# Low parts of the down projections' weights: subtraction on VectorE against negation and an adding transfer

## The chip, the cores and the metric

The kernel runs on one core of a Trainium2 chip. The metric is the device time of one execution in microseconds (us). A core has five engines with queues of their own: TensorE (PE; its weight loads are listed apart as PEld), VectorE (DVE), ScalarE (ACT), GpSimd (POOL) and SyncE (SP). Sixteen DMA engines serve the core. Each engine works through its own queue in order; semaphores tie the queues together.

## The reference

A decoder trunk of two layers over 256 tokens of width 1024, all in float32. Each layer adds three things to the residual stream `h`, and a final RMSNorm ends it:

```python
for l in range(DEPTH):                                        # DEPTH = 2
    h = h + 0.5 * swiglu(rmsnorm(h, ffn1_norm[l]), ffn1_w_gate[l], ffn1_w_up[l], ffn1_w_down[l])
    u = rmsnorm(h, mix_norm[l])
    z = u @ w_in[l]                                           # columns for three mixers and their gates
    ...                                                       # latent attention, differential attention, pooling
    h = h + merged @ w_out[l]
    h = h + 0.5 * swiglu(rmsnorm(h, ffn2_norm[l]), ffn2_w_gate[l], ffn2_w_up[l], ffn2_w_down[l])
return rmsnorm(h, final_norm)

def swiglu(x, w_gate, w_up, w_down):
    return (jax.nn.silu(x @ w_gate) * (x @ w_up)) @ w_down    # 1024 -> 2816 -> 1024
```

The down projection is the last product, 2816 by 1024. There are four of them: two in each layer.

## The kernel before

**Three products for one.** TensorE multiplies in the type `float32r`, which keeps fewer bits than float32. So each operand is split: `hi` is the value rounded to `float32r`, `lo` is what is left, `value - hi`. A product is made of three matmuls (`mm3`, lines 201 to 203): hi by hi, hi of the activations by lo of the weights (line 202), and lo of the activations by hi of the weights. The second of the three is the first that reads a weight tile's `lo`.

**Weight tiles.** All weights lie in one array, `wall`, in the order of use that `plan()` writes out by hand. A full tile is 4 blocks of 128 rows by 512 columns, in SBUF 128 partitions by 2048 values, 1024 KB. A down projection (names ending in `w_down`) has 22 blocks of rows and two halves of 512 columns: in each half five full tiles and one of two blocks (128 by 1024 values). So one down projection has 12 tiles, and the four have 48.

**The split of a tile** is `wsplit_now`. SyncE's queue loads the tile into `raw` (line 194). ScalarE rounds it into `hi` (line 183). VectorE subtracts, `lo = raw - hi` (line 184). For tiles of the feed-forward networks each of the two is one instruction for the whole tile. The first four tiles of the kernel take a path of their own (the branch `first`) and are no down projection's. `raw`, `hi` and `lo` have three buffers each, so a load waits until the tile three places earlier no longer needs its `raw`, and a cast until TensorE has finished with the `hi` of the tile three places earlier. Loads, casts and subtractions of the coming tiles run ahead of TensorE as far as these rings allow. `ahead()` issues one tile's split before the work behind which it would stand.

**The down projection** runs in `gemm_tokens`: for each half two accumulators of 128 tokens by 512 columns; for each tile four blocks, two token groups and three matmuls, 24 matmuls in a full tile. Its activations are `ghi` and `glo`, so that its matmuls appear in the profile as `acc<-hi,ghi`, `acc<-lo,ghi` and `acc<-hi,glo`. At the end of a half VectorE adds the result to `h` (line 369), and TensorE transposes it for the next norm. The last feed-forward of the kernel has no following norm; there the last two tiles of a half are taken together (`tail=2`), first one token group, then the other.

**GpSimd** has little to do in these stages: at the start of the next one it raises the norm's mean square to the power -1/2 (line 229). No transfer is issued from its queue.

Of the kernel before, what the change touches and what calls it, by code (L numbers as in the profile page):

```python
# [11 lines left out]
F32 = mybir.dt.float32  # L12
# [4 lines left out]
ALU = mybir.AluOpType  # L17
# [71 lines left out]
def trunk(ctx, tc, x, xt, positions, wall, small, lamrow, fnorm, out):  # L89
    nc = tc.nc  # L90
# [52 lines left out]
    def wsrc(spec):  # L143
        _, _, _, nk, _, n = spec
        return wall[offs[spec]:offs[spec] + P * nk * n].rearrange("(p k n) -> p k n", p=P, k=nk)
# [13 lines left out]
    def wsplit(spec):  # L159

        if spec not in pending_splits:
            pending_splits[spec] = wsplit_now(spec)
        return pending_splits.pop(spec)

    def ahead():

        i = order_of[latest[0]] + 1
        if i < len(order_of):
            spec = plan()[i]
            pending_splits[spec] = wsplit_now(spec)  # L170

    def wsplit_now(spec):
        latest[0] = spec
        _, _, _, nk, _, n = spec
        raw = wp.tile([P, nk, n], F32, tag="raw", name="raw")
        hi = wp.tile([P, nk, n], F32R, tag="hi", name="hi")
        lo = wp.tile([P, nk, n], F32R, tag="lo", name="lo")
        first = offs[spec] < 4 * P * 2048
        fl = lambda a: a.rearrange("p k n -> p (k n)")
        rawf, hif, lof = fl(raw), fl(hi), fl(lo)  # L180

        def split(ks):
            nc.scalar.copy(out=hif[:, ks], in_=rawf[:, ks])  # L183
            nc.vector.tensor_tensor(out=lof[:, ks], in0=rawf[:, ks], in1=hif[:, ks].bitcast(F32), op=ALU.subtract)  # L184

        if first:

            for k in range(nk):
                nc.sync.dma_start(out=raw[:, k], in_=wsrc(spec)[:, k])
                split(slice(k * n, (k + 1) * n))  # L190
                if opening:
                    opening.pop(0)()
            return hi, lo
        nc.sync.dma_start(out=raw, in_=wsrc(spec))
        step = nk * n // (1 if spec[0].startswith("ffn") else 2)
        for k in range(0, nk * n, step):
            split(slice(k, k + step))
        return hi, lo
# [611 lines left out]
    def last_half(n):  # L810
# [8 lines left out]
        for t in range(2):  # L819
# [4 lines left out]
            if n == 0:  # L824
# [13 lines left out]
                                                   in_=x[t * P:(t + 1) * P, n * 512:(n + 1) * 512])  # L838
# [67 lines left out]
```

## Time and profile before

| | |
|---|---|
| median of 2 runs | 1218.91 us (1218.87 to 1218.95) |
| the profiled execution's own time | 1219.01 us |
| its span, first to last instruction | 1217.2 us |
| granted TensorE clock | 0.999 |
| read from HBM | 210.85 MB |

The page gives busy time for each engine with its share of the span, the chain of work that ended last, and groups of equal instructions: line, engine, operation, output and inputs by the program's names, shapes, count; behind the bar busy time, mean ns of one, and the idle time before them with what ended most of it. Rows of waits read "engine, what it was about to make, its line <- what it waited for: us in total, times, longest". Rows of a timeline begin with the start and the duration in us. Rows of windows give each engine's busy time in a stretch, then the granted clock, the DMA engines' busy share and GB/s. Matmuls are pipelined, so one of 0.39 us starts every 0.23 us. "Share of 16 engines" is the time that a queue's packets took.

### The profile page before, as it was taken

What the parts mean: (1) busy time and instruction counts of PE and PEld (TensorE: products, weight loads), DVE (VectorE), ACT (ScalarE), POOL (GpSimd) and SP (SyncE); (2) the same over time, 40 slices, a digit from 0 to 9 for tenths busy, and PEclk for the clock granted to TensorE, in tenths of its full rate; (3) what the DMA queues carried; (4) which work ended last, traced back from release to release, by engine and by line L of the source; (5) the groups of instructions that cost most, each with busy time, mean ns of one, the idle gap of its engine ahead of it and who ended that gap; (6) DMA issues with size and microseconds to landing.
All of it is one profiled execution on the core that took longest, in us unless ns stands there. A gap on an engine that the chain in (4) does not pass through costs nothing.

```text
span 1217.2 us, 14925 instructions
## 1 busy us (share of the span) xinstructions
PE 1204.9 (99%) x5983; PEld 1007.9 (83%) x5983; DVE 721.0 (59%) x1046; ACT 570.2 (47%) x763; POOL 65.7 (5%) x126
## 2 busy tenths in 40 slices
PE   9999999999999999999999999999999999999997
PEld 6788889997788888888888888899877888888886
DVE  5665456777747655554554554568686485455553
ACT  6463444546544444443454443455465445444442
POOL 0000000600100000000000000034010000000000
PEclk9999999999999999999999999999999999999999
DMA  8554455234355555555555555544343554555541
GB/s 314 213 211 173 167 177 206 104 111 175 139 176 188 178 184 185 194 175 169 184 204 202 175 184 179 177 147 148 114 164 139 178 202 173 178 194 182 193 171 68
DMA packets 34613, 212.86 MB, mean 175 GB/s; under 512 B 4080, under 2 KB 5488, under 8 KB 10992
## 3 DMA queue, kind: packets, MB, share of 16 engines
q1 hardware_dynamic: 33408, 210.52, 49.2%
q10 hardware_dynamic: 1136, 1.40, 0.3%
q8 instruction: 47, 0.77, 0.2%
q14 instruction: 22, 0.18, 0.0%
HBM read 210.85 MB, written 1.05 MB: 174 GB/s over the span
## 4 chain that ended last, share of the span: by engine, by line
PE 94%; DVE 3%; issue 2%; ACT 1%; DMA 0%; SPq 0%; POOLq 0%; POOL 0%; DVEq 0%; ACTq 0%
PE acc L201 27%; PE acc L202 27%; PE acc L203 27%; PE o L641 2%; PE tr L316 2%; PE tr L203 1%; PE tr L201 1%; PE tr L202 1%; PE tr L607 1%; PE tr L634 1%; DVE lo L184 1%; PE tr L596 1%; PE tr L246 1%; DMA raw<-wall 0%; ACT hi L183 0%
## 5 line engine op out<-in xcount | busy, mean ns | idle before, releaser
L184 DVE TENSOR_TENSOR lo<-raw,hi 128x2048 fp32r<-128x2048 f32 (+4 forms) x284 | 465.0, 1650 | 387.7 <-ACT hi L183 387.5
L183 ACT CAST hi<-raw 128x2048 fp32r<-128x2048 f32 (+4 forms) x284 | 388.1, 1387 | 469.2 <-PE acc L203 379.6
L201 PE MATMUL acc<-hi,uhi 128*128 128x512 f32 (+1 forms) x896 | 350.9, 392 | 0.0
L202 PE MATMUL acc<-lo,uhi 128*128 128x512 f32 (+1 forms) x896 | 348.7, 389 | 1.9 <-DVE lo L184 1.8
L203 PE MATMUL acc<-hi,ulo 128*128 128x512 f32 (+1 forms) x896 | 348.1, 389 | 0.0
L202 PEld LDWEIGHTS acc<-lo,uhi 128*128 128x128 f32 x896 | 168.4, 188 | 35.8 <-DVE lo L184 2.5
L201 PEld LDWEIGHTS acc<-hi,uhi 128*128 128x128 f32 x896 | 168.2, 188 | 34.0 <-issue 1.5
L203 PEld LDWEIGHTS acc<-hi,ulo 128*128 128x128 f32 x896 | 168.2, 188 | 33.5
L201 PE MATMUL acc<-hi,ghi 128*128 128x512 f32 x352 | 137.7, 391 | 0.0
L203 PE MATMUL acc<-hi,glo 128*128 128x512 f32 x352 | 137.5, 390 | 0.0
L202 PE MATMUL acc<-lo,ghi 128*128 128x512 f32 x352 | 137.3, 390 | 0.0
L201 PEld LDWEIGHTS acc<-hi,ghi 128*128 128x128 f32 x352 | 66.1, 188 | 13.7
L203 PEld LDWEIGHTS acc<-hi,glo 128*128 128x128 f32 x352 | 66.1, 188 | 13.6
L202 PEld LDWEIGHTS acc<-lo,ghi 128*128 128x128 f32 x352 | 66.1, 188 | 13.5
L626 ACT ACTIVATE e<-e,mx 128x128 f32<-128x128 f32 (+1 forms) x96 | 42.7, 446 | 56.1 <-DVE mx L622 34.1
L201 PE MATMUL acc<-uhi,hi 128*128 128x256 f32 x192 | 55.6, 290 | 0.0
L202 PE MATMUL acc<-ulo,hi 128*128 128x256 f32 x192 | 55.2, 288 | 0.0
L203 PE MATMUL acc<-uhi,lo 128*128 128x256 f32 x192 | 55.0, 288 | 0.0
L357 ACT ACTIVATE sg<-acc,r 128x512 f32<-128x512 f32 (+1 forms) x48 | 31.2, 658 | 28.0 <-PE acc L203 28.0
L229 POOL TENSOR_TENSOR r<-r,mhalf 128x2 f32<-128x2 f32 x6 | 4.2, 703 | 707.4 <-DVE r L228 707.4
L201 PE MATMUL acc<-hi,y 128*128 128x512 f32 x96 | 37.7, 393 | 0.0
L203 PE MATMUL acc<-hi,y 128*128 128x512 f32 x96 | 37.4, 390 | 0.0
(201 smaller groups left out, 1224.6 us busy)
## 6 DMA issues: line engine op xcount, KB each, us to landing
raw<-wall SPq DMA_DIRECT2D x184, 1024.0 KB, 4.8
raw<-wall SPq DMA_DIRECT2D x10, 512.0 KB, 3.5
raw<-wall SPq DMA_DIRECT2D x18, 256.0 KB, 4.9
raw<-wall SPq DMA_DIRECT2D x4, 832.0 KB, 4.3
raw<-wall SPq DMA_DIRECT2D x2, 768.0 KB, 4.4
xT<-xt SPq DMA_DIRECT2D x8, 128.0 KB, 4.4
h<-x SPq DMA_DIRECT2D x4, 256.0 KB, 5.6
fn<-fnorm ACTq DMA_DIRECT2D x1, 512.0 KB, 5.4
```

Of the source, the lines that this page charges most:

```text
L183: nc.scalar.copy(out=hif[:, ks], in_=rawf[:, ks])
L184: nc.vector.tensor_tensor(out=lof[:, ks], in0=rawf[:, ks], in1=hif[:, ks].bitcast(F32), op=ALU.subtract)
L201: nc.tensor.matmul(ps, lhsT=lh, rhs=rh, start=start, stop=False)
L202: nc.tensor.matmul(ps, lhsT=lh, rhs=rl, start=False, stop=False)
L203: nc.tensor.matmul(ps, lhsT=ll, rhs=rh, start=False, stop=stop)
L246: nc.tensor.transpose(out=ps[:, (i * 2 + t) * P:(i * 2 + t + 1) * P], in_=h[:, t, k * P:(k + 1) * P], identity=ident)
L316: nc.tensor.transpose(out=ptr[:, (i * 2 + t) * P:(i * 2 + t + 1) * P], in_=g[t][:, (j + i) * P:(j + i + 1) * P], identity=ident)
L357: nc.scalar.activation(out=sg, in_=ps[0][t], func=AF.Silu, scale=r)
L596: nc.tensor.matmul(ps[:, i * nk:(i + 1) * nk], lhsT=qT[:, hd, qt * P:(qt + 1) * P], rhs=kT[:, hd, :nk], start=True, stop=True)
L607: nc.tensor.matmul(ps[m][:, i * nk:(i + 1) * nk], lhsT=dqT[a:a + 32, hd // 2, qt * P:(qt + 1) * P], rhs=dkT[a:a + 32, hd // 2, :nk], start ...
L626: nc.scalar.activation(out=e[:, sl], in_=e[:, sl], func=AF.Exp, bias=mx[:, i:i + 1], scale=-(2.0 ** -(hd + 1)) if slope else -1.0, accum_o ...
L641: nc.tensor.matmul(o[:, hd * 64:(hd + 1) * 64], lhsT=eT[:, j * P:(j + 1) * P], rhs=v[:, kt, hd * 64:(hd + 1) * 64], start=(kt == 0), stop= ...
```

## The change

For the tiles of the down projections the split is done in another way. ScalarE's rounding stays. VectorE writes the negated high part into `lo`, and a transfer issued from GpSimd's queue adds `raw` onto it, both in SBUF: `lo = -hi`, then `lo += raw`. TensorE's first use of `lo` then waits for this transfer, and so does the next load into the same `raw` buffer.

```diff
         nc.sync.dma_start(out=raw, in_=wsrc(spec))
+        if spec[0].endswith("w_down"):
+
+            nc.scalar.copy(out=hif, in_=rawf)
+            nc.vector.tensor_scalar(out=lof, in0=hif.bitcast(F32), scalar1=-1.0, scalar2=None, op0=ALU.mult)
+            nc.gpsimd.dma_start(out=lof, in_=rawf, accum_op=ALU.add)
+            return hi, lo
         step = nk * n // (1 if spec[0].startswith("ffn") else 2)
         for k in range(0, nk * n, step):
             split(slice(k, k + step))
```

## The prediction

> **What bounds the kernel now.** I read the busy shares of the page first, then the chain that ended last, then the waits.
>
> ```profile
> PE 1204.9 (99%) x5983; PEld 1007.9 (83%) x5983; DVE 721.0 (59%) x1046; ACT 570.2 (47%) x763; POOL 65.7 (5%) x126
> ...
> PE 94%; DVE 3%; issue 2%; ACT 1%; DMA 0%; SPq 0%; POOLq 0%; POOL 0%; DVEq 0%; ACTq 0%
> ```
>
> TensorE is busy for 1204.9 of 1217.2 us and carries 94% of the chain. What VectorE or ScalarE saves elsewhere is worth nothing unless TensorE waits for it. The waits show how little that is, and what the loads wait for:
>
> ```profile
> PE acc L202 <- DVE lo L184: 1.8, 1, 1.8
> ...
> PEld acc L202 <- DVE lo L184: 2.5, 2, 2.0
> ...
> SPq L194 <- DVE lo L184: 970.9, 181, 17.1
> ```
>
> The columns are total us, times and longest us. TensorE waited for a low part once, the weight loads twice: 4.3 us in all is the most that a quicker low part could return, 0.35%. The third row is the one to remember: SyncE's queue stands waiting for VectorE's `lo` nearly all the time, because a `raw` buffer comes free when the low part has been made. The loads are paced by buffers; the 16 DMA engines have room. How much room, by stage:
>
> ```profile
> core 0: us, PE busy (x) PEld busy (x) DVE busy (x) ACT busy (x) POOL busy (x), PEclk, DMA share, GB/s
> ...
> 6.00:12.00 6.00, 5.88 (x25) 4.03 (x23) 5.66 (x14) 3.09 (x5) 0.00 (x0) 1.00 1.04 352
> 12.00:30.00 18.00, 18.00 (x82) 14.80 (x80) 10.33 (x22) 14.71 (x24) 0.72 (x1) 1.00 0.92 355
> 134.00:196.00 62.00, 62.00 (x281) 51.00 (x280) 28.92 (x23) 25.35 (x27) 0.00 (x0) 1.00 0.52 179
> ...
> raw<-wall SPq DMA_DIRECT2D x184, 1024.0 KB, 4.8
> ```
>
> At the start the DMA engines are full (share about 1) and move 352 to 355 GB/s. A 1024 KB tile (1.049 MB) is therefore 2.95 us of all 16 engines; it lands 4.8 us after issue, so some 1.85 us is fixed. The third window is the first down projection (feed-forward 1 of layer 0), with TensorE busy throughout and DMA share 0.52.
>
> Its pace comes from the timeline of that stage, ScalarE's, VectorE's and TensorE's rows:
>
> ```profile
> 122.33 1.92 ACT L183 CAST hi<-raw 128x2048 fp32r<-128x2048 f32 x1 [3.53 <-PE acc L203]
> ...
> 140.14 1.91 ACT L183 CAST hi<-raw 128x2048 fp32r<-128x2048 f32 x1 [3.22 <-PE acc L203]
> 145.58 1.91 ACT L183 CAST hi<-raw 128x2048 fp32r<-128x2048 f32 x1 [3.53 <-PE acc L203]
> ```
>
> ```profile
> 124.28 2.29 DVE L184 TENSOR_TENSOR lo<-raw,hi 128x2048 fp32r<-128x2048 f32 x1 [1.20 <-ACT hi L183]
> ...
> 142.09 2.29 DVE L184 TENSOR_TENSOR lo<-raw,hi 128x2048 fp32r<-128x2048 f32 x1 [2.73 <-ACT hi L183]
> ```
>
> ```profile
> 134.25 0.39 PE L202 MATMUL acc<-lo,ghi 128*128 128x512 f32 x1
> ...
> 151.05 0.39 PE L202 MATMUL acc<-lo,ghi 128*128 128x512 f32 x1
> ...
> 195.06 0.39 PE L203 MATMUL acc<-hi,glo 128*128 128x512 f32 x1
> ```
>
> ScalarE's casts stand 5.44 us apart (140.14, 145.58), each released by TensorE's last matmul of the tile three places earlier: TensorE uses a full tile in 5.44 us, and three buffers make the ring. Tile 0 of the stage is cast at 122.33, its low part begun at 124.28 and first read at 134.25; tile 3 is cast at 140.14, begun at 142.09 and read at 151.05. The stage's last matmul ends at 195.45.
>
> **The change, part by part.** It touches 48 tiles: four stages of 40 full and 8 half tiles together, 11 full-tile equivalents in each. No other tile changes path.
>
> Removed: 48 subtractions on VectorE. Added: 48 negations on VectorE and 48 adding transfers from GpSimd's queue. The prices of the VectorE part:
>
> ```profile
> L184 DVE TENSOR_TENSOR lo<-raw,hi 128x2048 fp32r<-128x2048 f32 x124 | 284.0, 2291 | 282.5 <-ACT hi L183 282.5
> ...
> L263 DVE TENSOR_SCALAR uhi<-xT,sm 128x256 fp32r<-128x256 f32 x8 | 2.6, 350 | 3.9 <-DMA sm<-small 2.1 <-DMA xT<-xt 1.8
> ...
> L829 DVE TENSOR_SCALAR of<-of,r 128x512 f32<-128x512 f32 x2 | 1.0, 488 | 1.3 <-POOL r L828 1.3
> ```
>
> A one-input scalar operation grows by 138 ns per 256 columns (350 to 488), so 2048 columns are some 0.21 + 8 x 0.138 = 1.32 us, at most the subtraction's 2.29. I take 1.32. VectorE saves about 1 us a tile; off the path, that is worth nothing but an earlier start of the transfer.
>
> The transfer: no row shows one that adds, nor one from GpSimd's queue. Counted by bytes it reads `raw`, reads `lo` and writes `lo`, where a load reads once and writes once. Low end: the second read is free, 2.95 us of the engines. Next: each byte read costs what a load's byte costs, 2 x 2.95 = 5.90 us. High end: the three passes do not overlap, 8.85 us. I take 5.90, since at the saturated windows the engines gave 355 GB/s and had nothing left for a second stream. A cost below nothing is excluded, because 1 MB more is moved than before.
>
> What it does to the stage. After the change a tile needs 2.95 + 5.90 = 8.85 us of the DMA engines against TensorE's 5.44. The DMA engines become the bound. The sum for the first stage: tile 0's negation ends at 124.28 + 1.32 = 125.6. From there, until the last transfer has landed, the engines owe 11 x 5.90 = 64.9 us of transfers, and loads. Loads of tiles 0 to 2 are done by then (three `raw` buffers); eight full-tile equivalents are left, 23.6 us, and up to two loads for the next stage come between (0 to 4.8, I take 2.4). To that come 1.85 us fixed and the last half tile's matmuls, 2.7. That gives 95.5 us and an end at 221.1 instead of 195.45: +25.6. Four stages: +102. The very last stage takes its last two tiles as one part, with the order by row block, so 2.7 us more of matmuls lie behind the last landing: +105 in all. GpSimd's issue time lies beside the queue of transfers as long as the DMA engines are busy; if that cover is gone, 48 issues come to light, 16 us at SyncE's price and 79 us at that of GpSimd's longest row:
>
> ```profile
> L194 SPq DMA_DIRECT2D raw<-wall x16: 327/328/332, 121.2 to 199.4; - x16
> ...
> L229 POOL TENSOR_TENSOR hs<-hs,mhalf 128x8 f32<-128x8 f32 x4 | 6.6, 1654 | 199.1 <-DVE hs L228 199.1
> ```
>
> Added waits: TensorE's second matmul of each tile waits for a landing instead of VectorE. GpSimd's queue waits for the negation; behind it stands only the next stage's power for the norm factor. SyncE's queue waits for the landing before it reloads `raw`, and every later load stands behind that. At the stage's end this stays covered: tile 9's landing precedes tile 11's by 8.85 us or more, enough for the next load (4.8 us) and its split.
>
> The profiled execution took 1219.01 us (span 1217.2, and 1.8 around it), 0.1 above the median of the runs. 1219 + 105 = **1324 us**.
>
> By the Trainium skill, Collectives: The Full Stack, section "The bandwidth ceiling: the fold count and why AG ≠ RS ≠ AR", an add in the DMA engines is slow only through its two source reads on one ring, about 31 GB/s per engine halved; no run here shows it yet. An estimate from that page, 16 engines at 15.5 GB/s, makes the transfer 4.2 us, and my sum by it would be 77 us a stage, +7, in all some 1250.
>
> **The rivals.**
>
> *It stays hidden: not slower.* The mechanism is the three-buffer ring on `lo`. From the negation's end (142.09 + 1.32) to the reading of tile 3 (151.05) are 7.6 us. If a transfer lands as a load does (4.8 us) and costs the engines one pass, TensorE never stops. It decides at two points: landing under 7.6 us, and engine time under 3.6 us (11 x 3.6 + 30.55 = the 69.85 us between 125.6 and 195.45). For it: DMA share of 0.52. Against: one pass is already 2.95 + 2.95 = 5.9 in 5.44. It gives 1219, at best 1215. Chance 0.13.
>
> *The ring's latency bounds, not the engines' throughput.* With cheap bytes but a landing of 10 us (issue, 1.85 fixed, two reads, waiting behind a load), the ring gives 1.91 + 1.32 + 10 + 5.44 in three tiles, 6.22 a tile: +0.78 x 11, and 1.3 for the first one, +10 a stage, 1261. Chance 0.15.
>
> *Three passes one after another,* 8.85 us a transfer: 97.4 + 30.55 = 128 us, end at 253.5, +58 a stage, 1454; with GpSimd's issues in the open 1533. Nothing in the page shows such slow bytes; the operation is merely unseen. Chance 0.17.
>
> *Far worse:* the start's 256 KB loads took 5.6 us each to land; a megabyte at that pace, with no overlap, is 22.4 us:
>
> ```profile
> h<-x SPq DMA_DIRECT2D x4, 256.0 KB, 5.6
> ```
>
> 11 x 22.4 + 2.7 puts the stage's end at 375, and the whole near 1937. Those loads shared full engines, so this is remote. Chance 0.05.
>
> *TensorE slows when it waits.* Every window above shows a granted clock of 1.00, and no wait over 2 us. If gaps brought the clock to one half, a tile would take 10.9 us, more than the transfer's 8.85: +60 a stage, 1458. Chance 0.06. The Trainium skill, TensorE: Matmul & The Clock Gate, section "What's actually happening", has the clock fall to half after an idle window of about 3.4 us; no run here shows it.
>
> **How the numbers follow.** Forecast 1324, own range 1314 (no load for the next stage in between: 4 x 2.4 less) to 1403 (all of GpSimd's issues in the open: 79 more), chance 0.44. The range reaches from 1243, where the hidden case ends, to 1533, leaving out 0.13 below and 0.05 above. Two per cent, 24 us, is about what a measurement of this kernel can tell from no change. Slower by over 2%: 0.86 (the forecast and the other four rivals, 0.87, less the 0.01 for faster); same 0.13, the hidden case; faster 0.01, since 4.3 us is all there is to win.
>
> **What would show it.** In the changed profile's windows of the down projections: DMA share near 1 (0.52 now), TensorE's waits at the second matmul put down to the transfer's landing, casts some 8 to 9 us apart instead of 5.44, SyncE's queue waiting for GpSimd's transfer. The negation at 1.3 us shows the VectorE step. TensorE's busy time outside those windows unchanged. I am wrong if the DMA share stays well under 1 while TensorE waits (then latency or the add itself bounds), if the granted clock drops, or if the casts keep 5.44 us.

## The result, and the profile after

The changed kernel takes 1318.19 us (median of 2 runs, 1316.06 to 1320.32) against 1218.91: a ratio of 1.0815, 95% interval 1.0739 to 1.089. The forecast was 1324. The profiled execution took 1316.06 us, span 1314.2, so 1314.2 - 1217.2 = 97.0 us of span are to be found. Lines have moved: the cast, the negation and the transfer are 197 to 199, the three matmuls 207 to 209.

The page of the changed kernel: engine busy time, DMA queues, the chain that ended last, and DMA issues.

```profile
PE 1233.0 (94%) x5983; PEld 1021.1 (78%) x5983; DVE 675.8 (51%) x1046; ACT 569.8 (43%) x763; POOL 107.4 (8%) x174
...
q1 hardware_dynamic: 33408, 210.52, 45.0%
q0 software_dynamic: 6912, 46.14, 18.0%
...
PE 68%; DMA 21%; DVE 4%; issue 4%; ACT 3%; SPq 0%; POOL 0%; POOLq 0%; ACTq 0%; DVEq 0%
...
lo<-raw POOLq DMA_DIRECT2D x40, 1024.0 KB, 10.0
```

DMA was 0% of the chain and is 21%. The new queue q0 is GpSimd's. It moved 46.14 MB (44 full-tile equivalents; the second read is not counted) in 18.0% of the engines' time: 0.180 x 1314.2 / 44 = 5.38 us of all 16 engines for each full tile. By the same sum q1's share is 2.95 us for each 1.049 MB. A full tile's transfer lands 10.0 us after its issue (median).

The waits of SyncE's queue, and then those of the engines, in the changed kernel:

```profile
SPq L194 <- DMA lo<-raw: 333.9, 45, 13.5
```

```profile
ACT hi L197 <- DMA raw<-wall: 135.5, 27, 14.6
...
PE acc L208 <- DMA lo<-raw: 66.3, 23, 8.0
```

Read together, the three rows are one loop: SyncE's loads wait for a landing, ScalarE's casts wait for the loads, TensorE waits at its second matmul for the next landing. TensorE's books close nearly: 66.3 us of waiting and 1233.0 - 1204.9 = 28.1 us of longer matmuls make 94.4 of the 97.0.

Windows of the changed kernel; columns as before (engines, granted clock, DMA share, GB/s). The first is the first down projection, the second and third parts of it, the last two the end of the kernel's last one, when no loads are left:

```profile
134.00:220.00 86.00, 69.27 (x283) 55.26 (x282) 19.74 (x23) 25.20 (x26) 8.50 (x10) 0.90 0.97 253
...
145.00:160.00 15.00, 10.93 (x36) 8.42 (x35) 2.93 (x3) 3.24 (x3) 1.70 (x2) 0.77 1.03 252
160.00:180.00 20.00, 12.75 (x56) 9.94 (x55) 5.19 (x6) 6.34 (x5) 3.38 (x4) 0.91 0.95 251
...
1291.00:1293.00 2.00, 1.89 (x5) 1.50 (x6) 0.00 (x0) 0.00 (x0) 0.00 (x0) 0.50 0.97 197
1293.00:1296.00 3.00, 3.00 (x9) 2.32 (x8) 0.00 (x0) 0.00 (x0) 0.00 (x0) 0.50 1.03 208
```

The DMA share went from 0.52 to 0.97 over the stage: the engines are full. In the last two windows, where adding transfers have the engines to themselves at a share of about 1, they move only 197 to 208 GB/s of result, where loads moved 352 to 355 in the kernel before. A second thing stands in the clock column: 0.77, and 0.50 at the end. The timeline shows how it comes about, and where the stage ends:

```profile
145.57 0.39 PE L207 MATMUL acc<-hi,ghi 128*128 128x512 f32 x1
150.03 0.79 PE L208 MATMUL acc<-lo,ghi 128*128 128x512 f32 x1 [4.07 <-DMA lo<-raw]
150.62 0.63 PE L209 MATMUL acc<-hi,glo 128*128 128x512 f32 x1
...
218.84 0.39 PE L209 MATMUL acc<-hi,glo 128*128 128x512 f32 x1
```

After a wait of 4.07 us the matmuls take 0.63 us instead of 0.39. The stage ends at 219.2; the forecast had 221.1. From the first to the last matmul with a low part the four stages took 60.5, 60.6, 60.6 and 59.7 us before and take 84.2, 81.8, 82.9 and 85.6: together +93.1.

### The profile page after: what moved, and what is told of

The parts are those of the page before. It is cut to its first block, busy times and chain, and to the rows that moved or that the text cites. A ratio compares the mean times of both kernels' runs of the same rounds, so it can differ in the third digit from the quotient of the medians.

```text
span 1314.2 us, 15028 instructions
## 1 busy us (share of the span) xinstructions
PE 1233.0 (94%) x5983; PEld 1021.1 (78%) x5983; DVE 675.8 (51%) x1046; ACT 569.8 (43%) x763; POOL 107.4 (8%) x174
## 3 DMA queue, kind: packets, MB, share of 16 engines
q0 software_dynamic: 6912, 46.14, 18.0%
HBM read 210.85 MB, written 1.05 MB: 161 GB/s over the span
## 4 chain that ended last, share of the span: by engine, by line
PE 68%; DMA 21%; DVE 4%; issue 4%; ACT 3%; SPq 0%; POOL 0%; POOLq 0%; ACTq 0%; DVEq 0%
PE acc L208 19%; PE acc L207 19%; PE acc L209 19%; DMA lo<-raw 11%; DMA raw<-wall 10%; PE o L647 2%; ACT hi L197 2%; DVE lo L184 1%; PE tr L207 1%; PE tr L209 1%; PE tr L208 1%; PE tr L322 1%; PE tr L613 1%; DVE lo L198 1%; PE tr L640 1%
## 5 line engine op out<-in xcount | busy, mean ns | idle before, releaser
L184 DVE TENSOR_TENSOR lo<-raw,hi 128x1024 fp32r<-128x1024 f32 (+3 forms) x236 | 363.8, 1556 | 303.2 <-ACT hi L183 303.0
L183 ACT CAST hi<-raw 128x1024 fp32r<-128x1024 f32 (+3 forms) x236 | 303.6, 1311 | 355.6 <-PE acc L209 227.3
L208 PE MATMUL acc<-lo,ghi 128*128 128x512 f32 x352 | 148.3, 421 | 66.3 <-DMA lo<-raw 66.3
L197 ACT CAST hi<-raw 128x2048 fp32r<-128x2048 f32 (+1 forms) x48 | 84.8, 1767 | 195.9 <-DMA raw<-wall 135.5
L198 DVE TENSOR_SCALAR lo<-hi 128x2048 fp32r<-128x2048 f32 (+1 forms) x48 | 54.6, 1138 | 206.4 <-ACT hi L197 206.4
L209 PE MATMUL acc<-hi,glo 128*128 128x512 f32 x352 | 145.1, 412 | 0.0
L207 PE MATMUL acc<-hi,ghi 128*128 128x512 f32 x352 | 144.4, 411 | 0.0
L208 PEld LDWEIGHTS acc<-lo,ghi 128*128 128x128 f32 x352 | 70.8, 201 | 90.7 <-DMA lo<-raw 75.9
L199 POOL DMA_DIRECT2D lo<-raw x48 | 41.6, 867 | 655.5 <-DVE lo L198 624.1
L209 PEld LDWEIGHTS acc<-hi,glo 128*128 128x128 f32 x352 | 70.9, 202 | 14.2
```

What stands on the lines that cost most here:

```text
L197: nc.scalar.copy(out=hif, in_=rawf)
L198: nc.vector.tensor_scalar(out=lof, in0=hif.bitcast(F32), scalar1=-1.0, scalar2=None, op0=ALU.mult)
L199: nc.gpsimd.dma_start(out=lof, in_=rawf, accum_op=ALU.add)
L207: nc.tensor.matmul(ps, lhsT=lh, rhs=rh, start=start, stop=False)
L208: nc.tensor.matmul(ps, lhsT=lh, rhs=rl, start=False, stop=False)
L209: nc.tensor.matmul(ps, lhsT=ll, rhs=rh, start=False, stop=stop)
```

## The experiments

**The theory:** the 16 DMA engines set the pace, 2.95 us of load and 5.4 of adding transfer against TensorE's 5.44, and the transfer is dear, as I reason, because it reads twice. **The rivals:** the landing time around the rings of three buffers; GpSimd's queue in itself; the half clock after gaps; the negation. Later expectations build on the earlier results. "The first stage" below is the first down projection.

### One part alone: the negation

```diff
-            nc.gpsimd.dma_start(out=lof, in_=rawf, accum_op=ALU.add)
```

> The adding transfer is left out, so lo stays -hi; the negation stays. Theory (the DMA engines are over-booked by the transfer: 2.9 us for a load plus 5.3 for the add per tile against TensorE's 5.44): without it nothing is slow, 1215 to 1223 us, casts of the down projections 5.44 us apart again. Rival (three-buffer ring and landing time): the same, since the landing is gone too. If the negation itself, or ScalarE's order of work, had a share, over 1230.

Measured 1218.72 us, ratio 0.9998 (0.9989 to 1.0008). The negation, its order on VectorE and SyncE's earlier release cost nothing. All of the loss belongs to the transfer.

### The transfer without its add

```diff
-            nc.gpsimd.dma_start(out=lof, in_=rawf, accum_op=ALU.add)
+            nc.gpsimd.dma_start(out=lof, in_=rawf)
```

> The transfer from GpSimd's queue stays, with its waits, but copies raw into lo and does not add, so lo is raw. Theory (bytes read by the engines): one read instead of two, about 2.9 us of the 16 engines instead of 5.4, some 63 us of work in a stage's 70, so 1219 to 1240 us. Rival (landing time of a transfer from GpSimd's queue, whatever it carries, around the ring of three): landing stays near 9 to 10 us and the time at 1280 to 1320.

Measured 1252.48 us, ratio 1.0278 (1.0261 to 1.0296). The page and the waits of this run:

```profile
q0 software_dynamic: 6912, 46.14, 10.0%
...
lo<-raw POOLq DMA_DIRECT2D x40, 1024.0 KB, 6.4
```

```profile
ACT hi L197 <- DMA raw<-wall: 47.5, 13, 7.0
...
PE acc L208 <- DMA lo<-raw: 22.0, 13, 4.0
```

The engine time is as expected: 0.100 x 1250.1 / 44 = 2.84 us a tile, so the add is 5.38 / 2.84 = 1.89 copies. The queue itself is not what is dear: a copy from it takes the engines 2.84 us, a load from SyncE's queue 2.95. An add from another queue was not run. Two thirds of the loss (66 of 99 us) went with it, and landing fell to 6.4. But 34 us stayed, 12 more than my theory allowed, and the time lies in neither range. TensorE still waited, though a median landing of 6.4 us is inside the 7.6 that the ring covers.

### Two copies in place of one add

```diff
-            nc.gpsimd.dma_start(out=lof, in_=rawf, accum_op=ALU.add)
+            nc.gpsimd.dma_start(out=lof, in_=rawf)
+            nc.gpsimd.dma_start(out=spare[:, :nk * n], in_=rawf)
```

> The add is left out (lo is raw), and the same bytes are copied a second time into a spare tile, so that the engines make two copies instead of one add of two reads. Theory (the add costs what its reads cost, 1.9 copies by the queue's share): about 5.7 us of the engines per tile, loads behind both landings, 1300 to 1345 us. Rival (adding in the engines is slow by itself, not by its second read): two copies at 2.8 us each overlap freely, 1252 to 1285 us.

Measured 1315.97 us (1313.08 to 1324.4), ratio 1.081 (1.077 to 1.085): the changed kernel's time, 1318, by another route. Its page, and its window over the first stage:

```profile
q0 software_dynamic: 13824, 92.28, 18.0%
```

```profile
134.00:195.00 61.00, 51.26 (x200) 40.20 (x199) 13.41 (x16) 18.21 (x18) 8.31 (x15) 0.89 0.96 360
```

Twice the packets and bytes, the same 18.0%, and 360 GB/s where the adding kernel shows 256 in the same window, at a share of 0.99. The engines are as full in both. An add costs the engines what two copies cost. That the second read is the reason is not shown: two copies make two reads and also two writes. The equal share is firmer than the equal time, for this run has a wait of its own: `spare` is a single tile, and GpSimd's queue stood 121.1 us in all until the copy before had landed in it.

### Full engines or waiting loads: four buffers for raw

```diff
-        raw = wp.tile([P, nk, n], F32, tag="raw", name="raw")
+        raw = wp.tile([P, nk, n], F32, tag="raw", name="raw", bufs=4)
...
```

The same is done in `wraw`, the other place that makes a `raw`.

> Nothing is left out; raw has four buffers instead of three, so a load waits for the transfer of the tile four places earlier. Theory: the engines are full in the stage (share 0.97), so the pace stays: 1300 to 1322 us. Rival (ring): ScalarE waited 135 us for loads that stood behind landings; with a ring of four most of that goes, 1230 to 1275 us.

Measured 1297.12 us (1293.21 to 1301.17), ratio 1.064 (1.0614 to 1.0666). The wait and the window over the first stage:

```profile
ACT hi L197 <- DMA raw<-wall: 6.3, 2, 5.5
```

```profile
134.00:195.00 61.00, 52.41 (x211) 41.97 (x211) 14.63 (x17) 20.12 (x19) 7.22 (x9) 0.89 1.01 260
```

The casts no longer wait for loads (135.5 to 6.3 us), and 21 us return, 3 more than the theory's range allowed. The other 78 stay, with the engines at a share of 1.01. So by this run the ring of `raw` had a part, about a fifth; the rest stays while the engines are full.

### Loads that wait for no landing: the add from HBM

```diff
-            nc.gpsimd.dma_start(out=lof, in_=rawf, accum_op=ALU.add)
+            nc.gpsimd.dma_start(out=lof, in_=fl(wsrc(spec)), accum_op=ALU.add)
```

> Nothing is left out; the transfer adds the tile from HBM instead of from raw, so raw is free after the cast and no load waits for a landing. Theory: the same bytes over the same engines, 1300 to 1345 us (HBM as a slower source at most). Rival (raw's ring and SyncE's queue behind landings): 1230 to 1270 us.

Measured 1309.32 us (1305.61 to 1314.87), ratio 1.0744 (1.0713 to 1.0774). SyncE now waits for the cast, and the DMA share over the first stage is 1.03:

```profile
SPq L194 <- ACT hi L197: 278.8, 45, 13.6
```

Taking the transfer off SyncE's path while its engine time stays (0.177 x 1306.0 / 44 = 5.25 us) returns 9 us of 99. That fits the theory and not the ring as the main cause. It is less than the 21 of the fourth buffer; landing rose to 12.0 us with the source in HBM, and what that takes back was not separated. So the ring's part is not known more closely than these two figures.

### The other half of the load taken away

```diff
...
+        if down:
+            raw = once[0][:, :nk]
...
-        nc.sync.dma_start(out=raw, in_=wsrc(spec))
+        if not down:
+            nc.sync.dma_start(out=raw, in_=wsrc(spec))
```

All the down projections' tiles take their values from one tile, `once`, which is loaded a single time.

> The loads of the down projections' tiles are left out but one: all 48 tiles use that tile's data, and cast, negation and adding transfer stay. Theory: the engines have 5.3 us of adds for each 5.44 of TensorE, landing falls to about 7 us: 1217 to 1245 us, GB/s near 200 in the stages. Rival (the add's landing stays near 10 us whatever else runs): (1.91 + 1.23 + 10 + 5.44) / 3 = 6.2 us a tile, 1255 to 1275 us. If the add were slower by itself than 5.44 us: over 1275.

Measured 1236.74 us, ratio 1.0146 (1.0131 to 1.0161), as expected. The page's queue and issues, and the waits:

```profile
q0 software_dynamic: 6912, 46.14, 18.7%
...
lo<-once POOLq DMA_DIRECT2D x40, 1024.0 KB, 7.1
```

```profile
PE acc L217 <- DMA lo<-once: 12.0, 11, 2.1
```

With the adds still made but the stage's loads gone, landing falls from 10.0 to 7.1 us and 82% of the loss is gone, while the engines' time for a transfer is nearly what it was: 0.187 x 1234.6 / 44 = 5.25 us. Neither the load nor the transfer is too much for the engines; their sum is. By itself this run does not part the theory from the ring of `raw`, since without loads that ring is gone too; the two runs before it do.

### Half as many transfers

```diff
-        if spec[0].endswith("w_down"):
+        if spec[0].endswith("w_down") and spec[2] % 8 == 0:
```

> Nothing is left out; only every other tile of the down projections (6 of 12 in a stage, all full ones) goes by negation and adding transfer, the rest by the subtraction. Theory: 6 x 5.4 + 26 of loads + 4.5 = 63 us of work in a stage's 70: hidden, 1217 to 1240 us. Rival (each landing of 10 us against the 7.6 the ring covers): 6 stalls of 2.4 us a stage, 1250 to 1280 us.

Measured 1256.06 us, ratio 1.0295 (1.0274 to 1.0317): a miss, inside the rival's range. The page's issues, the wait, the window over the first stage, and the three waits of TensorE in it:

```profile
lo<-raw POOLq DMA_DIRECT2D x24, 1024.0 KB, 8.8
...
PE acc L208 <- DMA lo<-raw: 22.1, 15, 2.5
...
134.00:195.00 61.00, 55.84 (x240) 44.59 (x238) 19.50 (x18) 21.33 (x21) 4.25 (x5) 0.97 0.86 242
...
146.44 0.50 PE L208 MATMUL acc<-lo,ghi 128*128 128x512 f32 x1 [0.96 <-DMA lo<-raw]
159.65 0.50 PE L208 MATMUL acc<-lo,ghi 128*128 128x512 f32 x1 [2.03 <-DMA lo<-raw]
170.50 0.50 PE L208 MATMUL acc<-lo,ghi 128*128 128x512 f32 x1 [2.17 <-DMA lo<-raw]
```

The DMA share is 0.86, so here the engines are not full throughout. Landing is 8.8 us, above the 7.6. TensorE's books close again: 22.1 us of waits and 1213.4 - 1204.9 = 8.5 us of longer matmuls make 30.6 of the 31.8 us by which this execution's span is longer. So below full engines a second term decides: single landings that come late, and the slower matmuls behind them.

### Is it the loads' ring? Two runs with a fourth raw buffer

The plain copy and the every-other-tile kernel, each with `bufs=4` for `raw`.

> The transfer copies and does not add, so lo is raw, as in the run with the plain copy (1252 us, DMA share 0.84 in the stage); raw has four buffers. Theory as it stands now (two terms: engines over-booked where the sum exceeds TensorE's time, and the raw ring, where load 7 us + 1.9 + 1.2 + landing 6 to 8 us exceeds three tiles of 5.44): with full engines out of the way the ring is what is left of the 34 us, and a fourth buffer takes it away: 1219 to 1230 us. Rival (what is left is the waiting of TensorE for single late landings, whatever the loads do): 1243 to 1253 us.

> Nothing is left out; every other tile of the down projections by negation and adding transfer, as in the run at 1256 us, with four buffers for raw. In that run no cast of the stage waited for a load; TensorE waited 1 to 2 us at an adding tile, landing 8.8 us. Theory (ring of lo: landing over 7.6 us): the fourth raw buffer changes little, 1245 to 1258 us. Rival (the raw ring): 1219 to 1235 us.

The copy: 1246.86 us, ratio 1.0245 (1.0218 to 1.0272), not the 1219 to 1230 expected but inside the rival's 1243 to 1253. Every other tile: 1255.43, ratio 1.0298 (1.026 to 1.0336), unchanged, as expected. So the loads' ring is at most 6 us of what is left in the copy, and nothing that shows in the other. The copy with four buffers still shows one long wait in its first stage:

```profile
169.18 0.80 PE L208 MATMUL acc<-lo,ghi 128*128 128x512 f32 x1 [2.99 <-DMA lo<-raw]
```

### Landing in two halves

Negation and transfer are made in two halves of a tile's columns: every other tile with three raw buffers, and then all 48 tiles with four.

```diff
...
+            m = nk * n // 2
+            for a in (slice(0, m), slice(m, nk * n)):
+                nc.vector.tensor_scalar(out=lof[:, a], in0=hif[:, a].bitcast(F32), scalar1=-1.0, scalar2=None, op0=ALU.mult)
+                nc.gpsimd.dma_start(out=lof[:, a], in_=rawf[:, a], accum_op=ALU.add)
...
```

> Nothing is left out; every other tile by negation and adding transfer as in the run at 1256 us, but each tile's negation and transfer in two halves of the columns, so that TensorE can start on the first two blocks while the second half is under way. Theory (what is left there is the landing, 8.8 us against the 7.6 that the ring covers, with the engines not full): the first half lands in about 6 us and the second is needed 2.7 us later, 1219 to 1236 us. Rival (loads and transfers contend, and whatever finishes late finishes late): 1248 to 1258 us.

> Nothing is left out; all 48 tiles by negation and adding transfer, in two halves each, and four buffers for raw: all that the experiments offer against waiting. Theory (full engines: 2.8 of load and 5.4 of add for each 5.44 of TensorE): 1285 to 1300 us, near the 1297 of four raw buffers alone. Rival (landings still set the pace there): 1240 to 1275 us.

Every other tile: 1253.85 us, ratio 1.0295 (1.0278 to 1.0312), a miss again, inside the rival's range. The small waits of its first stage are gone and one long wait stands in their place. Below its row stands GpSimd's issue of the two halves that it waits for:

```profile
169.83 0.79 PE L210 MATMUL acc<-lo,ghi 128*128 128x512 f32 x1 [4.82 <-DMA lo<-raw]
...
159.02 1.73 POOL L201 DMA_DIRECT2D lo<-raw  x2 [9.15 <-DVE lo L200]
```

It stands at the tile behind the half tile of the first column half. That tile is cast at 156.09 and its first transfer issued at 159.02; when it is cast, TensorE has one full tile and one half ahead of it, 8.2 us instead of 10.9. That shorter cover explains at most 2.7 of the 4.82 us. The landing was late as well: TensorE went on 10.8 us after the issue, where the median of this run's halves is 7.8. And the halves cost the loads something: ScalarE's casts at line 183 waited 72.6 us for them, against 19.2 with whole transfers. This reading is argued from the timeline; no run varied the half tile alone, so the cause of the 28 to 37 us that stay in these runs is open in its parts.

All 48 tiles: 1288.01 us, ratio 1.0574 (1.0558 to 1.059), as the theory expected, with the engines' share at 1.05:

```profile
134.00:195.00 61.00, 53.15 (x221) 42.11 (x220) 15.19 (x26) 20.73 (x20) 15.49 (x18) 0.94 1.05 263
```

This is the best that the change reached with all 48 tiles, still 69 us slower than the kernel before. No experiment pointed to a version quicker than that kernel.

### The clock

```diff
...
+            for _ in range(10 if fill else 0):
+                nc.tensor.matmul(pf, lhsT=idle[:, :P], rhs=idle, start=True, stop=True)
...
```

> Nothing is left out; before each tile of the down projections TensorE runs ten idle matmuls (2.3 us at full clock) into an unused bank, so that its gaps stay short. Theory: the granted clock (0.77 to 0.91 in these stages) goes back to 1.00 and the time stays within 1305 to 1330 us, because the engines set the pace; at most 10 us are returned where TensorE works after the last landing. Rival (TensorE's half clock after gaps is a large part of the loss): 1270 to 1300 us.

Measured 1327.74 us, ratio 1.0892 (1.0874 to 1.0911). The granted clock is back at 1.00 with the engines still full:

```profile
134.00:195.00 61.00, 60.74 (x273) 42.70 (x277) 12.33 (x16) 18.11 (x18) 5.94 (x7) 1.00 0.99 252
```

But the run decides nothing. Between the first and the last matmul with a low part lie eleven full tiles' worth of matmuls and eleven groups of fillers, 11 x (5.44 + 2.27) = 84.8 us of TensorE, and its first stage took 85.6: the fillers were a bound of their own, so a gain under them could not have shown. How much of the 28.1 us of longer matmuls lies on the path is open.

## Why the prediction was right, step by step

- **What binds.** The claim that the engines become the bound held: share 0.97 over the first stage and 0.91 to 1.03 in the windows within it, where 0.52 had stood; 1316 us with two copies in place of the add; 1237 without loads; 1297, 1309 and 1288 where waits were eased and bytes were not.
- **The transfer's price.** I took two loads' worth, 5.90 us, between 2.95 and 8.85. It measured 5.38, two copies' worth of 2.69 to 2.84. The choice was right and 10% high. By the Trainium skill, Collectives: The Full Stack, section "The bandwidth ceiling: the fold count and why AG ≠ RS ≠ AR", it is the two source reads that make an add dear, said there of ReduceScatter; its measured ratio, 1.93, is that of AllGather's bandwidth to ReduceScatter's. The traces agree in the ratio, 1.89, and leave the reason open. The estimate worked out from that page, 4.2 us, was too low, and so was the 1250 it led to.
- **The sum.** With 5.38 in place of 5.90 a stage's sum falls by 5.7 us, and the whole becomes 1324 - 4 x 5.7 = 1301. That is near what the kernel with four raw buffers shows, 1297. The step that failed is the statement that the loads behind the landings stay covered: SyncE's loads stood behind the landings, and casts waited 135.5 us for them, worth 21 us by the fourth buffer and 9 by the add from HBM. By the first figure two errors of about 22 us each cancelled. That is luck: 1324 against 1318 looks better than the working was. Longer matmuls, 28.1 us in all, were no term of the sum either.
- **The negation.** Forecast 1.32 us, at most 2.29. Its row:

```profile
L198 DVE TENSOR_SCALAR lo<-hi x48: 694/1227/1229, 124.5 to 1287.4; 128x2048 fp32r<-128x2048 f32 x40, 128x1024 fp32r<-128x1024 f32 x8
...
L199 POOL DMA_DIRECT2D lo<-raw x48: 843/862/1052, 126.3 to 1288.4; - x48
```

  1.23 us, and worth nothing in time. GpSimd's issue is 0.86 us and lies beside full engines, as assumed.
- **The pace.** Casts were to come 8 to 9 us apart. They do so only in part; from the stage's tile 2 on they stand at 134.73, 143.37, 150.64 and 158.43, later ones up to 18 us apart:

```profile
143.37 1.91 ACT L197 CAST hi<-raw 128x2048 fp32r<-128x2048 f32 x1 [6.26 <-DMA raw<-wall]
150.64 1.90 ACT L197 CAST hi<-raw 128x2048 fp32r<-128x2048 f32 x1 [5.36 <-DMA raw<-wall]
...
193.44 1.92 ACT L197 CAST hi<-raw 128x2048 fp32r<-128x2048 f32 x1 [8.00 <-PE acc L209]
```

- **The clock.** I named a falling clock as a sign of being wrong and gave that rival 0.06. It fell, to 0.77 in one window and 0.50 in another, and the time did not follow to 1458. TensorE's matmuls lengthened by 28.1 us in all; how much of that cost time is open.
- **The hidden case.** Its two conditions were a landing under 7.6 us and engine time under 3.6. The plain copy met both by its medians (6.4 and 2.84) and still lost 34 us. The condition was too kind: it took one landing for every tile, where the copies' went from 2.9 to 10.4 us, and one cover for all, where the timeline has less behind the half tile.

## What to carry to other kernels

Do not price a transfer by its result alone (an adding one took two copies' worth here), and add it to the loads of the same stage before calling the DMA engines idle: here a share of 0.52 left 0.48 x 5.44 = 2.6 us a tile, less than the 2.84 of one plain copy of the same data. Work moved off an engine that does not bind returns nothing (the subtraction's 1 us a tile), while the resource it moves to may become the bound. A transfer placed inside a ring of buffers lengthens the ring twice, for the reader of its result and for whoever reloads its source; check the shortest cover of the ring, not the usual one.

## What the runs showed of the hardware that was not expected

- An add of 1.049 MB from GpSimd's queue takes 5.38 us of the 16 engines (5.25 with the stage's loads left out), the same as two plain copies (2 x 2.69), and 197 to 208 GB/s of result is all it reached alone. Landing has a median of 7.1 us with the loads left out, 10.0 beside them.
- The clock's fall does not follow a wait's length alone, nor at once. In the copy with four raw buffers it came with the first matmul after a wait of 2.99 us (0.80 us, shown above), and after a wait of 3.91 us, over which it was granted in full, only some 2 us into the work that followed:

```profile
590.80 0.50 PE L208 MATMUL acc<-lo,ghi 128*128 128x512 f32 x1 [3.91 <-DMA lo<-raw]
591.14 0.40 PE L209 MATMUL acc<-hi,glo 128*128 128x512 f32 x1
...
592.73 0.78 PE L209 MATMUL acc<-hi,glo 128*128 128x512 f32 x1
```

  The Trainium skill, TensorE: Matmul & The Clock Gate, section "What's actually happening", lets the clock fall to half by how busy TensorE has been; its table asks for one idle window of about 3.4 us. A fall after 2.99 us without matmuls (3.31 without weight loads) is earlier than that, and here the measurement decides; the drop to 0.50 itself agrees.
